# Sixty-four-row matmuls widened to 128 rows in a hybrid attention and convolution encoder

## The chip, the cores and the metric

The kernel runs on one core of a Trainium2 chip. The metric is the device time of one execution in microseconds; lower is better. On the core, TensorE multiplies (PE in the rows; its weight loads are listed apart, as PEld), VectorE (DVE), ScalarE (ACT) and GpSimd (POOL) work elementwise, SyncE (SP) issues the transfers, and 16 DMA engines carry them out.

## The reference

Two requests, of 512 and of 1024 tokens, pass through the same two layers:

```
h = rms_norm(x); proj = h @ w_in            # 1024 -> 3328 columns
q, k, v, g_a, u_h, g_h = split(proj)
attn: 8 query heads, 2 key heads, head size 64; q and k normalised and rotated
      s = q @ k.T * scale;  p = softmax(s);  o = p @ v
o_a = rms_norm(attn) * silu(g_a)
hyena: two long convolutions per channel, whose filters come from a small network:
      h = sin(fr * (z @ w1 + b1)); h = sin(fr * (h @ w2 + b2)); h = h @ w3   # 64 -> 2048
      h = h * (exp(-t * |decay|) + 0.05), normalised, then used through transforms
o_h = rms_norm(conv result) * silu(g_h)
x = x + concat(o_a, o_h) @ w_out
```

Two products have an inner size of 64: the scores `q @ k.T` (head size 64) and the third filter layer `h @ w3` (64 hidden units).

## The kernel before

Each operand of a product is kept as two 16-bit numbers, a high half and a low half (what the high half left over). A product of two such operands is three products of halves, high by high, high by low and low by high, added up in PSUM; low by low is left out.

Where the inner size is 64, the 128 partitions are used to do two of the three at once. `q_chunk` stores queries of key head g with their high half in the 64 partitions that start at g*64 and their low half in the other 64. `kv_chunk` stores the high half of each key head twice, one copy in each half of the partitions. So in `scores` the first matmul of a key block works on 128 rows (line 922: high and low queries by high keys), and the second on 64 rows alone (line 923: high queries by low keys). Line 923 occurs 320 times in the program. The third filter layer does the same in `filter_gen`, lines 801 and 802, with features stacked high over low and `w3_tile` giving the weights; line 802 occurs 96 times. All matmuls are issued by one helper, line 346, so all have that line in the rows. A row calls a matmul by its weight tile's rows and columns (`64*128` is a matmul on 64 rows) and by its moving operand (`64x512`).

The keys of one block of 512 tokens are built in `t16`, 12 tiles of 128x128 (four token tiles by three slots: head 0 high, head 1 high, low of both), and one transposing transfer on SP's queue (line 663) turns them into `kT`, 3 KB a partition. Queries go the same way with 16 tiles (line 629), softmax weights with 8 or 16 (line 945).

The work is cut into parts, which three threads walk through in a fixed order (`THREADS`): projections of both layers, filters and then attention, convolution and output of the long request, attention and the rest of the short one. `emit` writes the program down by turns from these threads, keeping an estimate of VectorE's work near a set ratio to TensorE's; each engine then works in that order. On-chip memory is handed out by `Arena` in pieces of 1 KB a partition, by age. When fewer than `ROOM` = 32 of its 202 KB are free, `emit` lets only the first thread go on (a thread that found itself waiting excepted):

```python
            tight = self.m.n - sum(self.m.used) < ROOM
            for t in order:
                if tight and n > 1 and t is not threads[0] and threads[0].last != "wait":
                    continue
```

Attention makes a tile of scores for 128 queries, takes its softmax (maximum on DVE, exponential on ACT, two halves on ACT and DVE, a transposing transfer), and multiplies by the values some tiles later.

Of the kernel before, what the change touches and what calls it, by code (L numbers as in the profile page):

```python
# [13 lines left out]
AF = mybir.ActivationFunctionType  # L14
ALU = mybir.AluOpType
AX = mybir.AxisListType.X

P = 128
# [11 lines left out]
RATIO = 0.85  # L30
# [17 lines left out]
# column offsets of the per-channel parameters  # L48
C_NW, C_CW, C_CB, C_DEC, C_HB, C_AW, C_HW, C_N = 0, 8, 44, 56, 72, 80, 84, 88

S_H = 2.0 ** 10      # normalised activations
S_W = 2.0 ** 8       # projection weights
S_QK = 2.0 ** 7      # q and k after rotation
S_V = 2.0 ** 8
S_P = 2.0 ** 14      # softmax weights
S_C = 2.0 ** 11      # transform matrices
S_F = 2.0 ** 13      # filters
S_OA = 2.0 ** 8      # gated attention output
S_OH = 2.0 ** 10     # gated hyena output
S_U = (2.0 ** 6, 2.0 ** 8)   # folded conv inputs  # L60
S_Y = (2.0 ** 5, 2.0 ** 7)   # spectra of conv outputs
S_W3 = 2.0 ** 10
# [79 lines left out]
class Arena:  # L142
    """On-chip memory in units of 1 KB a partition. A piece is taken that has been free for a while, small
    short-lived ones from the low end and the others from the high end; if there is none, the piece that has
    been free for longest."""
# [41 lines left out]
class Psum:  # L187
    """PSUM banks by class of use; in each class the banks free for longest are taken first."""
# [29 lines left out]
class Thread:  # L218
    """Parts of the work in their order, as steps."""
# [14 lines left out]
class Kern:  # L234
# [24 lines left out]
    def share(self, name, load):  # L259
        """Buffers that several threads read: loaded by the first, freed by the last."""  # L260
        if name not in self.shared:
            self.shared[name] = [load(), 0]
        self.shared[name][1] += 1
        return self.shared[name][0]
# [10 lines left out]
    def keep(self, n):  # L275
        """Columns that stay."""
        o = self.small_n
        self.small_n += n
        assert self.small_n <= 512
        return self.small[:, o:o + n]  # L280

    def tmp(self, n):
        """Columns that are soon used up."""
        if self.ring_n + n > 512:
            self.ring_n = 0
        o = self.ring_n
        self.ring_n += n
        return self.ring[:, o:o + n]
# [7 lines left out]
    def early(self, ap):  # L296
        """Instructions that free a PSUM bank go before others of their time."""
        return EVAC if ap.tensor is self.pt_tensor else 0
# [54 lines left out]
    def emit(self, threads):  # L353
        """Emit threads side by side, so that the work of VectorE keeps to RATIO times that of TensorE: by
        turns one whose present part loads TensorE more, or one whose present part loads VectorE more."""
# [31 lines left out]
    def rsqrt(self, out, ss, n, a, b):  # L387
        """out = (a * ss + b) ** -0.5 on [P, n] columns."""
        v, y, z = self.tmp(n), self.tmp(n), self.tmp(n)
        self.ts(v, ss, a, b, ALU.mult, ALU.add)  # L390
        yi = y.bitcast(I32)
        self.ts(yi, v.bitcast(I32), 1, None, ALU.logical_shift_right)
        self.ts(yi, yi, -1, 0x5F3759DF, ALU.mult, ALU.add)
        for i in range(3):
            self.tt(z, y, y, ALU.mult)
            self.stt(z, z, -0.5, v, ALU.mult, ALU.mult)
            self.stt(out if i == 2 else y, z, 1.5, y, ALU.add, ALU.mult)

# [18 lines left out]
    def sine(self, out, x, n):  # L417
        """out = sin(x) with x taken into [-pi, pi]."""
        b = self.m.alloc((n * 4 + 1023) // 1024)
        k = b.f32(n)  # L420
        magic = 12582912.0
        self.ts(k, x, 1.0 / (2 * math.pi), magic, ALU.mult, ALU.add)
        self.ts(k, k, magic, None, ALU.subtract)
        c1 = 6.28125
        c2 = float(np.float32(2 * math.pi - c1))
        for c in (c1, c2):
            self.stt(x, k, -c, x, ALU.mult, ALU.add)
        self.ts(x, x, 3.1415925, -3.1415925, ALU.min, ALU.max)
        self.act(out, x, AF.Sin)
        b.free()  # L430

    def features(self):
        """Hidden layers of the filter networks, one layer of the trunk in each half of the partitions;
        each is stored as a stack of a high and a low half."""
# [110 lines left out]
    def w_chunk(self, l, c0):  # L545
        """256 columns of w_in, scaled and split; the halves are kept in memory for the next use."""
# [19 lines left out]
    def tok_proj(self, l, w, blk, done):  # L566
        """Four token tiles of 256 output columns, handed to done two at a time."""
# [17 lines left out]
    def rotate(self, raw, nh, blk, kind):  # L585
        """raw [P, 4, nh * 64]: per-head RMS norm and rotation in place of the tile; returns its Buf."""
# [26 lines left out]
    def q_chunk(self, l, blks, g):  # L613
        """Four query heads of one key head."""
# [19 lines left out]
    def kv_chunk(self, l, blks):  # L634
        W, w = self.w_chunk(l, 512)
        m = self.m
        for blk in blks:
# [15 lines left out]
            tb = m.alloc(3)  # L653
            t16 = tb.f16(1536)
            for g in range(2):
                hi = V(t16, g * 128, [384, 4], [64, 2], [1, 64])
                src = V(rb.f32(512), g * 64, [128, 4], [0, 2], [1, 64])
                self.act(hi, src, AF.Copy, scale=S_QK)
                self.stt(V(t16, 256 + g * 64, [384, 4], [1, 64]), V(rb.f32(512), g * 64, [128, 4], [1, 64]), S_QK,
                         V(t16, g * 128, [384, 4], [1, 64]), ALU.mult, ALU.subtract)  # L660
            rb.free()
            kb = self.kT[l, blk] = m.alloc(3, True)
            self.q.dma_start_transpose(out=V(kb.f16(1536), 0, [P, 12], [1, P]), in_=t16)
# [4 lines left out]
    def ch_proj(self, l, w, c2, blk):  # L668
        """One tile of 128 output channels over one block of tokens."""
# [10 lines left out]
    def u_chunk(self, l, blks, j):  # L680
        """Short convolution of 256 channels."""
# [27 lines left out]
    def g_chunk(self, l, blks, j):  # L709
        """Gates, as silu times 2 * S_H * S_W."""  # L710
# [17 lines left out]
    def proj_q(self, l, s):  # L728
        """Queries, keys, values and their gates."""
# [11 lines left out]
    def proj_u(self, l, s):  # L741
        """Inputs of the convolutions and their gates."""
# [29 lines left out]
    def w3_tile(self, l, o, c):  # L772
        """Columns of filt_w3 for 128 channels, forward and backward; the high half twice, the low half once."""
# [6 lines left out]
        self.stt(w[0:64, 1], r[0:64], S_W3, w[0:64, 0], ALU.mult, ALU.subtract)  # L780
# [3 lines left out]
    def filter_gen(self, l, o, c, w3, F, t, L, t0):  # L784
        """Windowed filters of 128 channels, forward and backward, with their scale."""
        m = self.m
        out = []
        for dr in range(2):
# [7 lines left out]
            for i in range(L // 512):  # L796
# [5 lines left out]
                self.mm(p.ap, w3[0:64, 1, ch:ch + P], F[0:64, r], False, True)  # L802
# [79 lines left out]
    def attention(self, l, s):  # L882
        """Score tiles run one ahead of the softmax, products with V one behind it."""
# [31 lines left out]
    def scores(self, l, blks, qg, pr, j, qi):  # L915
# [3 lines left out]
        for i, kb in enumerate(blks):  # L919
            kt = self.kT[l, kb].f16(1536).rearrange("p (t s n) -> p t s n", t=4, s=3)  # L920
            o = s.ap[:, i * 512:(i + 1) * 512]
            self.mm(o, qv, kt[:, :, g], True, False)
            self.mm(o, qv[g * 64:g * 64 + 64], kt[g * 64:g * 64 + 64, :, 2], False, True)
        return s

    def softmax(self, s, PT, qi, nb):
        """Weights of one tile of 128 queries, normalised, split and transposed."""
# [20 lines left out]
    def values(self, l, blks, qg, pr, PT, sqs):  # L948
        """Weighted values of two heads for 256 queries, by channel, and their gate."""
# [34 lines left out]
    def gate_out(self, l, c, o, t0, n, sc, od, grp):  # L984
        """o [128 channels, n tokens] times its gate, split and stored for the output projection."""
# [53 lines left out]
    def conv_chain(self, l, s, c, CF, CI):  # L1039
        """Both convolutions of 128 channels of one sequence."""  # L1040
# [12 lines left out]
    def fold(self, u, dst, scale, nb):  # L1053
        """Sums and differences of the halves of each block about its middle, split and transposed."""
# [117 lines left out]
    def split(self, dst, y):  # L1172
        """High and low halves of y, which dst holds in its first free dimension."""
# [4 lines left out]
    def wo_tiles(self, l, grp):  # L1178
        """The rows of w_out of one group of heads, scaled and split."""
# [24 lines left out]
    def out_half(self, l, t, grp, x, sc, WO):  # L1204
        """x += sc * (gated group output) @ (its rows of w_out) for one token tile."""
# [15 lines left out]
    def out_attn(self, l, s):  # L1221
        """The attention heads' part of the output projection, added to the residual of one sequence."""
# [19 lines left out]
    def out(self, l, s):  # L1242
        """The other part of the output projection, and the norm that follows."""
# [75 lines left out]
def _layout(a):  # L1319
    """Per-channel parameters as columns, and the weights in the order of their loads."""  # L1320
# [32 lines left out]
```

## Time and profile before

| what | value |
|---|---|
| time, median of 3 runs | 2420.97 us (2419.26 to 2422.3) |
| profiled execution, first to last instruction (span) | 2406.2 us |
| instructions | 39740 |
| TensorE busy | 2061.8 us, 15436 matmuls, 15436 weight loads |
| VectorE busy | 1853.7 us |
| ScalarE busy | 1146.9 us |
| GpSimd busy | 432.0 us |
| mean granted TensorE clock | 0.940 of full speed |
| main DMA queue's packets | 78.6% of 16 engines' span |

The busy time of an engine is the time during which at least one of its instructions was under way. Matmuls overlap each other in the pipeline and their ends are modelled, so the distance from one start to the next says more than the duration of one.

### The profile page before, as it was taken

How to read it: one execution, taken by the hardware profiler on the slowest of the kernel's cores; microseconds unless marked ns; L12 is line 12 of the kernel's file. 1: busy time of each engine (PE TensorE's matmuls, PEld its weight loads, DVE VectorE, ACT ScalarE, POOL GpSimd, SP SyncE). 2: the span in 40 equal slices, each digit the busy share in tenths (PEclk: the TensorE clock that was granted, in tenths of full speed). 3: DMA queues.
4: the chain of work that ended last, by engine and by line, in shares of the span. 5: the costliest groups of instructions: out<-in, count | busy, mean ns of one | idle time of the engine just before them, and what ended most of it. 6: DMA issues, size and time to landing. Idle time of an engine off the chain costs nothing. (4 is left out here: it accounts for less than half of the span.)

```text
span 2406.2 us, 39740 instructions
## 1 busy us (share of the span) xinstructions
PE 2061.8 (86%) x15436; PEld 1249.0 (52%) x15436; DVE 1853.7 (77%) x3109; ACT 1146.9 (48%) x2016; POOL 432.0 (18%) x288
## 2 busy tenths in 40 slices
PE   5888889999989889878798778899999998887587
PEld 3656544444554556555575645444446445555453
DVE  7777677777767889976778767687777776998966
ACT  6545445766644234223544445366655652232322
POOL 1323120000110222222223312100011002222321
PEclk9899999999999899989899989999999999999789
DMA  8686659989999668688956678688989999574664
GB/s 230 151 209 174 166 152 216 225 187 203 230 253 265 189 171 215 193 260 266 222 137 191 169 184 215 177 195 192 225 187 197 225 264 305 173 202 118 204 203 136
DMA packets 774534, 485.86 MB, mean 202 GB/s; under 512 B 664838, under 2 KB 720295, under 8 KB 761288
## 3 DMA queue, kind: packets, MB, share of 16 engines
q1 hardware_dynamic: 773952, 482.96, 78.6%
q8 instruction: 121, 1.98, 0.3%
q14 instruction: 69, 0.57, 0.1%
q10 hardware_dynamic: 392, 0.34, 0.1%
HBM read 192.76 MB, written 139.20 MB: 138 GB/s over the span
## 5 line engine op out<-in xcount | busy, mean ns | idle before, releaser
L346 PE MATMUL psum<-arena 128*128 128x512 f16 (+4 forms) x15052 | 2018.5, 300 | 311.7 <-DMA arena<-arena 150.8
L346 PEld LDWEIGHTS <-arena 128*128 128x128 f16 (+2 forms) x15040 | 1199.0, 104 | 1087.5 <-issue 450.4
L328 POOL TENSOR_TENSOR arena<-arena 128x512 f32<-128x512 f32 (+4 forms) x218 | 415.2, 1912 | 1750.7 <-ACT arena L308 1032.4
L328 DVE TENSOR_TENSOR arena<-arena 128x1024 f32<-128x1024 f32 (+4 forms) x484 | 524.5, 1114 | 68.0 <-POOL arena L328 26.9
L308 ACT ACTIVATE arena<-arena 128x512 f16<-128x512 f32 (+4 forms) x359 | 265.1, 753 | 386.3 <-DVE arena L328 208.2
L320 DVE SCALAR_TENSOR_TENSOR arena<-arena,ring 128x1024 f16<-128x1024 f32 (+2 forms) x292 | 352.7, 1224 | 62.7 <-ACT arena L308 61.4
L308 ACT ACTIVATE arena<-psum 128x512 f32<-128x512 f32 (+2 forms) x336 | 177.2, 533 | 386.7 <-PE psum L346 380.6
L308 ACT ACTIVATE arena<-arena,ring 128x1024 f16<-128x1024 f32 (+1 forms) x280 | 287.2, 1044 | 148.9 <-DVE ring L939 29.8
L340 DVE TENSOR_REDUCE ring<-psum 128x1 f32<-128x1024 f32 (+1 forms) x192 | 197.5, 1039 | 55.6 <-PE psum L346 55.4
L308 ACT ACTIVATE arena<-arena,small 128x256 f16<-128x256 f32 (+5 forms) x288 | 167.2, 628 | 143.5 <-DMA arena<-in_p_win_dram 27.0
L320 DVE SCALAR_TENSOR_TENSOR arena<-psum,small,arena 128x511 f32<-128x511 f32 (+2 forms) x240 | 173.4, 743 | 63.8 <-PE psum L346 42.0
L320 DVE SCALAR_TENSOR_TENSOR arena<-psum,arena 128x512 f32<-128x512 f32 (+2 forms) x188 | 107.4, 598 | 129.7 <-ACT arena L308 121.0
L308 ACT ACTIVATE arena<-psum,ring 128x1024 f32<-128x1024 f32 (+1 forms) x192 | 185.6, 967 | 5.0 <-DMA g<-arena 0.5
L320 DVE SCALAR_TENSOR_TENSOR arena<-arena,small 128x256 f16<-128x256 f32 (+1 forms) x224 | 123.5, 583 | 22.9 <-ACT arena L308 15.2
L320 DVE SCALAR_TENSOR_TENSOR arena<-arena 128x512 f32<-128x512 f32 (+5 forms) x135 | 119.4, 890 | 11.7 <-ACT arena L308 11.1
L320 DVE SCALAR_TENSOR_TENSOR arena<-arena,psum 128x512 f32<-128x512 f32 (+1 forms) x144 | 95.6, 679 | 29.4 <-PE psum L346 15.2
L308 ACT ACTIVATE ring<-ring 128x1 f32<-128x1 f32 x192 | 37.4, 197 | 124.7 <-DVE ring L340 124.1
L334 DVE TENSOR_SCALAR ring<-ring 128x1 f32<-128x1 f32 (+8 forms) x339 | 61.1, 184 | 40.5 <-ACT arena L308 37.9
L308 ACT ACTIVATE arena<-psum,small 128x512 f32<-128x512 f32 x72 | 55.3, 771 | 53.7 <-PE psum L346 53.2
L346 PE MATMUL psum<-small,arena 128*128 128x1 f32 x384 | 56.5, 264 | 21.6 <-ACT arena L308 20.3
L346 PEld LDWEIGHTS psum<-small,arena 128*128 128x128 f32 x384 | 56.4, 218 | 33.9 <-ACT arena L308 24.2
L320 DVE SCALAR_TENSOR_TENSOR ring<-ring 128x16 f32<-128x16 f32 (+3 forms) x238 | 45.9, 194 | 5.0
(29 smaller groups left out, 262.9 us busy)
## 6 DMA issues: line engine op xcount, KB each, us to landing
f<-arena SPq DMA_DIRECT2D x128, 256.0 KB, 3.1
arena<-in_p_win_dram SPq DMA_DIRECT2D x26, 1024.0 KB, 6.2
w<-arena SPq DMA_DIRECT2D x26, 1024.0 KB, 4.7
arena<-w SPq DMA_DIRECT2D x26, 1024.0 KB, 6.1
arena<-f SPq DMA_DIRECT2D x16, 1536.0 KB, 7.4
u<-arena SPq DMA_DIRECT2D x24, 512.0 KB, 3.4
arena<-o SPq DMA_DIRECT2D x48, 256.0 KB, 4.2
y<-arena SPq DMA_DIRECT2D x24, 512.0 KB, 5.3
```

The lines of the kernel that those rows point to most:

```text
L308: r = self.s.activation(out=out, in_=in_, func=func, scale=scale, **kw)
L320: r = self.v.scalar_tensor_tensor(out=out, in0=a, scalar=sc, in1=b, op0=op0, op1=op1)
L328: r = (eng or self.v).tensor_tensor(out=out, in0=a, in1=b, op=op)
L334: return (eng or self.v).tensor_scalar(out=out, in0=a, scalar1=s1, scalar2=s2, op0=op0, **kw)
L340: r = self.v.tensor_reduce(out=out, in_=in_, op=op, axis=AX, **kw)
L346: return self.pe.matmul(out, lhsT, rhs, start=start, stop=stop)
```

## The change

Low halves are kept twice too, so that the third product also works on all 128 partitions. `t16` gets a fourth slot (the low half of each head in a slot of its own, in both halves of the partitions), `tb` and `kT` go from 3 to 4 KB, the transfer from 12 to 16 tiles, and one more ACT instruction a head copies the low half into the other 64 partitions' columns. In the filter the low half of `w3` is computed for all 128 rows, which already hold two copies. Lines 802 and 923 take all 128 rows; by that they also add low by low. The rest of the diff takes out comments and leaves the lines where they were.

```diff
@@ kv_chunk
-            tb = m.alloc(3)
-            t16 = tb.f16(1536)
+            tb = m.alloc(4)
+            t16 = tb.f16(2048)
             for g in range(2):
-                hi = V(t16, g * 128, [384, 4], [64, 2], [1, 64])
-                src = V(rb.f32(512), g * 64, [128, 4], [0, 2], [1, 64])
-                self.act(hi, src, AF.Copy, scale=S_QK)
-                self.stt(V(t16, 256 + g * 64, [384, 4], [1, 64]), V(rb.f32(512), g * 64, [128, 4], [1, 64]), S_QK,
-                         V(t16, g * 128, [384, 4], [1, 64]), ALU.mult, ALU.subtract)
+                src = V(rb.f32(512), g * 64, [128, 4], [1, 64])
+                hi, lo = (V(t16, (i * 2 + g) * 128, [512, 4], [1, 64]) for i in range(2))
+                self.act(V(t16, g * 128, [512, 4], [64, 2], [1, 64]), V(rb.f32(512), g * 64, [128, 4], [0, 2], [1, 64]), AF.Copy, scale=S_QK)
+                self.stt(lo, src, S_QK, hi, ALU.mult, ALU.subtract)
+                self.act(V(t16, (2 + g) * 128 + 64, [512, 4], [1, 64]), lo, AF.Copy)
             rb.free()
-            kb = self.kT[l, blk] = m.alloc(3, True)
-            self.q.dma_start_transpose(out=V(kb.f16(1536), 0, [P, 12], [1, P]), in_=t16)
+            kb = self.kT[l, blk] = m.alloc(4, True)
+            self.q.dma_start_transpose(out=V(kb.f16(2048), 0, [P, 16], [1, P]), in_=t16)
@@ w3_tile
-        self.stt(w[0:64, 1], r[0:64], S_W3, w[0:64, 0], ALU.mult, ALU.subtract)
+        self.stt(w[:, 1], r, S_W3, w[:, 0], ALU.mult, ALU.subtract)
@@ filter_gen
                 self.mm(p.ap, w3[:, 0, ch:ch + P], F[:, r], True, False)
-                self.mm(p.ap, w3[0:64, 1, ch:ch + P], F[0:64, r], False, True)
+                self.mm(p.ap, w3[:, 1, ch:ch + P], F[:, r], False, True)
@@ scores
-            kt = self.kT[l, kb].f16(1536).rearrange("p (t s n) -> p t s n", t=4, s=3)
+            kt = self.kT[l, kb].f16(2048).rearrange("p (t s n) -> p t s n", t=4, s=4)
             self.mm(o, qv, kt[:, :, g], True, False)
-            self.mm(o, qv[g * 64:g * 64 + 64], kt[g * 64:g * 64 + 64, :, 2], False, True)
+            self.mm(o, qv, kt[:, :, 2 + g], False, True)
```

## Rows read from the trace of the kernel before

**Rows 1.** Page, part 1: busy us (share of the span) x instructions.

```profile
PE 2061.8 (86%) x15436; PEld 1249.0 (52%) x15436; DVE 1853.7 (77%) x3109; ACT 1146.9 (48%) x2016; POOL 432.0 (18%) x288
```

**Rows 2.** Windows: length, busy (x) of PE PEld DVE ACT POOL, clock, DMA share, GB/s.

```profile
0.00:300.00 300.00, 236.66 (x2044) 164.89 (x2045) 226.63 (x447) 160.06 (x258) 69.79 (x65) 0.91 0.75 186
300.00:800.00 500.00, 460.44 (x3041) 242.03 (x3038) 366.32 (x655) 284.49 (x520) 52.35 (x39) 0.97 0.93 219
800.00:1500.00 700.00, 573.00 (x4753) 387.39 (x4752) 557.76 (x893) 293.55 (x494) 169.17 (x108) 0.92 0.74 198
1500.00:2000.00 500.00, 469.63 (x3047) 238.84 (x3044) 364.10 (x682) 295.38 (x566) 40.58 (x35) 0.99 0.88 209
2000.00:2406.00 406.00, 322.10 (x2559) 215.83 (x2559) 338.88 (x434) 113.39 (x178) 100.12 (x41) 0.91 0.62 190
```

**Rows 3.** Counts of the 64-row form in 300 to 800, then 1500 to 2000 us.

```profile
L346 PE MATMUL psum<-arena 64*128 64x512 f16 x157 | 60.7, 387 | 0.0
...
L346 PE MATMUL psum<-arena 64*128 64x512 f16 x166 | 64.2, 387 | 0.0
```

**Rows 4.** Chain that ended last: its first piece; by line, 1500 to 2000, 2000 to 2406.

```profile
1444.52 4.56 DVE arena L320 x2
...
by line: PE psum L346 58.6%; DMA arena<-arena 14.6%; DVE arena L320 9.0%; ACT arena L308 3.9%; DMA arena<-in_p_win_dram 2.6%; DVE ring L340 1.8%; issue 1.7%; SPq L945 1.5%; DMA f<-arena 1.2%; DMA u<-arena 0.9%; DMA arena<-u 0.9%; DVE arena 
...
by line: DVE arena L328 37.6%; PE psum L346 23.1%; DVE arena L320 11.7%; issue 7.4%; DMA arena<-f 5.7%; DMA arena<-arena 4.7%; ACT arena L308 3.0%; POOL arena L328 2.2%; DVE ring L320 1.2%; DMA arena<-o 0.8%; DVE ring L328 0.7%; DMA u<-aren
```

**Rows 5.** Groups by form, whole span: busy us, mean ns | idle before, releasers.

```profile
L346 PE MATMUL psum<-arena 128*128 128x512 f16 x4448 | 1104.1, 386 | 58.3 <-DVE arena L320 21.2 <-ACT arena L308 15.9 <-DMA arena<-o 7.6
L346 PEld LDWEIGHTS <-arena 128*128 128x128 f16 x12704 | 1043.2, 102 | 850.1 <-issue 248.5 <-ACT arena L308 50.8 <-DVE arena L328 31.8
...
L346 PE MATMUL psum<-arena 64*128 64x512 f16 x416 | 163.2, 393 | 0.0
...
L346 PEld LDWEIGHTS <-arena 64*128 64x128 f16 x416 | 38.4, 93 | 157.2 <-issue 156.2 <-DVE ring L334 0.4
...
L308 ACT ACTIVATE arena<-arena 128x256 f16<-128x256 f32 x64 | 26.1, 409 | 23.4 <-DVE arena L320 12.5 <-issue 5.5 <-DMA arena<-in_filt_w_dram 3.0
...
L320 DVE SCALAR_TENSOR_TENSOR arena<-arena 64x256 f16<-64x256 f32 x16 | 7.5, 470 | 1.0 <-ACT arena L308 1.0
...
L320 DVE SCALAR_TENSOR_TENSOR arena<-arena 128x256 f16<-128x256 f32 x12 | 5.0, 420 | 4.4 <-ACT arena L308 4.1
```

**Rows 6.** Timeline of matmuls, one unbroken run of a single form.

```profile
1006.24 2.10 PE L346 MATMUL psum<-arena 128*128 128x512 f16 x9
```

**Rows 7.** Timeline of weight loads in attention: start us, length, instruction, idle before.

```profile
1618.01 0.10 PEld L346 LDWEIGHTS <-arena 128*128 128x128 f16 x1 [0.23 <-issue]
1618.33 0.09 PEld L346 LDWEIGHTS <-arena 64*128 64x128 f16 x1 [0.23 <-issue]
1618.65 0.11 PEld L346 LDWEIGHTS <-arena 128*128 128x128 f16 x2 [0.23 <-issue]
```

**Rows 8.** Timeline of weight loads while filters are made.

```profile
189.21 0.09 PEld L346 LDWEIGHTS <-arena 64*128 64x128 f16 x1 [0.32 <-issue]
189.53 0.55 PEld L346 LDWEIGHTS <-arena 128*128 128x128 f16 x6 [0.23 <-issue]
```

**Rows 9.** Waits, whole span: total us, times, longest.

```profile
ACT arena L308 <- DVE arena L320: 133.6, 83, 5.6
```

**Rows 10.** Line 663, key transfers: issue ns min/median/max, who waited, landing us.

```profile
L663 SPq DMA_TRANSPOSE arena<-arena x6: 1481/2028/2410, 67.2 to 1838.2; - x6
...
ACT arena L308: 1.7, 1
...
DMA to landing us min/median/max: 4.0/6.1/6.8
```

**Rows 11.** Line 629, query transfers of 16 tiles: issue ns, landing us.

```profile
L629 SPq DMA_TRANSPOSE arena<-arena x12: 1322/2872/5727, 136.5 to 1905.5; - x12
...
DMA to landing us min/median/max: 4.3/4.8/9.1
```

## The prediction

> **What bounds the kernel now.** I read the busy shares first, then the windows by stage, then the chain of waits, and last the timeline of single weight loads. The shares name no sole bound: TensorE is busy 2061.8 us and VectorE 1853.7 of a span of 2406.2 [rows 1]. The windows show stages with different limits [rows 2]. In the two stretches where attention of the long request runs beside projections, 300 to 800 and 1500 to 2000 us, TensorE is busy 460 and 470 of 500 us and VectorE 366 and 364: there TensorE leads, with 30 to 40 us of true idleness. From 800 to 1500 both are near 80%, and at the end VectorE leads. Of the 416 matmuls on 64 rows, 157 and 166 lie in the two TensorE-led stretches [rows 3]; the other 93 lie before 300 us and from 800 to 1500, most of them in the filters.
>
> Busy is not the same as deciding. The chain of waits, which the trace follows back no further than 1444 us, says how much of a stretch TensorE decides: 58.6% between 1500 and 2000 us, and 23.1% at the end [rows 4]. Transposing transfers (14.6%) and VectorE take most of the rest of the attention stretch, and while the chain passes through them TensorE is mostly busy with something that nothing waits for. A saving there becomes a wait.
>
> **What a 64-row matmul costs.** The group rows mislead here: 393 ns for one on 64 rows against 386 for one on 128 [rows 5]. That is a modelled time through the pipeline, which says nothing of how soon the next starts. The reader should look at starts. A run of nine 128-row matmuls over 512 columns takes 2.10 us in all [rows 6]; less one duration of 0.386 that leaves eight steps of 0.214 us. In the scores the loads alternate 128, 64, 128 rows and start at 1618.01, 1618.33 and 1618.65 [rows 7]: steps of 0.32 us, with an idle 0.23 us before each load that is put down to "issue" and to no other engine. In the filters the step behind a 64-row load is again 0.32 us (189.21 to 189.53) [rows 8]. So both the step into 64 rows and the step out of them cost 0.32 instead of 0.214 us, and one 64-row matmul costs 2 x 0.32 - 2 x 0.214 = 0.21 us more than one on 128 rows would. The group of loads agrees: 156 us of idle "issue" stand before 416 loads of 64 rows, 0.375 us each [rows 5], which includes the normal gap.
>
> Some switches stand beside a wait, which hides them, so I take 0.20 us: 416 x 0.20 = 83 us of TensorE time. The bounds are 0 (the wider matmul might keep the long step) and 416 x 0.21 = 87.
>
> **Two readings of the 0.32 us.** It could be a weight load that nothing covers: 0.102 us for a load [rows 5] and 0.214 for the columns make 0.316. Or it could be a price of changing between 128 and 64 rows. In the unbroken run above every matmul has a load of its own, since loads and matmuls are equal in number [rows 1], and it still steps at 0.214 us, so between matmuls of one shape the load is covered. The widened matmuls have that shape, so I take the second reading; the first is a rival below. The Trainium skill, TensorE: Matmul & The Clock Gate, Part 3 (The mechanism), speaks for the first: a weight load overlaps a matmul in flight only where the row groups differ. By that rule the step of equal shapes would be 0.316 us and the change would give nothing; the plain run at 0.214 us disagrees. The same skill, TensorEngine Tiling (Array Packing), Key Properties, speaks for the second: changing the tiling mode drains TensorE. By that rule the sum stays as it is, and the 0.32 us on both sides of a 64-row matmul agree.
>
> **The parts.**
> - *Lines 923 and 802 on 128 rows*: 83 us less on TensorE. On the path: 323 matmuls in the attention stretches are 64.6 us. TensorE decides 58.6% of a stretch in which it is busy 93.9%, so 0.586 / 0.939 = 0.62 of its work is on the chain [rows 2, 4]. The chain is not shown for 300 to 800 us; its busy shares are within 2 points of the other's, and I use the same 0.62. That is 64.6 x 0.62 = 40.3 us. For the 93 others, 18.6 us, the nearest chain is that of the last, mixed stretch: 0.231 / 0.793 = 0.29 [rows 2, 4], so 5.4 us. Together 45.7.
> - *The copies of the low keys*: six calls of the key part (three blocks, two layers) with two copies each, 12 ACT instructions. The nearest row, 256 columns to 16 bits, has 0.409 us [rows 5], so 4.9 us of ACT. Each copy also waits for VectorE's low half (0.42 us, [rows 5]) while the next head's high half and the evacuation of projection banks stand behind it on ACT; a wait of ACT for this line of VectorE is 133.6 / 83 = 1.6 us on average [rows 9]. The upper bound is 12 x (0.41 + 1.6) = 24 us, the lower 0. ACT has 3.9% of the chain [rows 4] and is under 60% busy in every stage [rows 2], which hides nearly all of it: I take 2 us. Without that cover it would be the 24.
> - *The key transfer*, 12 to 16 tiles: the query transfers have just that size and land in 4.8 us against 6.1 for the keys [rows 10, 11], so no price for size can be seen in the landing. SP's issue takes 2.87 us against 2.03 [rows 10, 11]: 6 x 0.84 = 5 us more on SP's queue, in front of whatever the program issues next. Only one wait, of 1.7 us by ACT, hangs on the key transfers [rows 10], and SP's queue has 1.5% of the chain [rows 4]: 0, at most 5.
> - *VectorE's low half of w3* on 128 instead of 64 partitions: 0.47 us now, and 0.42 for 256 columns on 128 partitions [rows 5]; 16 instructions, 0 give or take 1 us.
> - *Memory*: 1 KB more for each key block, while blocks are live. It changes where pieces lie and when the order of emission thinks memory tight. No row prices it; see the last rival.
>
> The sum is -45.7 + 2 = -43.7 us. The profiled span of 2406.2 becomes 2362.5. Between that span and the median of the runs, 2421.0, lie 14.8 us outside the first and last instruction, which I keep: 2377 us.
>
> **The rivals.**
> - *All of it arrives.* If TensorE's order alone sets the pace, as its 92 to 94% in the attention stretches could mean, 83 us are saved less the 2: 2340 us. Against it are the 14.6% of transfers and 9% of VectorE on the chain [rows 4].
> - *It turns into waits.* Scores come earlier, but the softmax chain and its transposing transfer set when values may start. DMA engines are busy 0.93 and 0.88 of the attention stretches [rows 2], the highest of all stages, so transfers asked for sooner may land no sooner. If only a quarter of the 83 us arrives, 2421 - 21 + 2 = 2402 us; if none, 2421. For it: the chain is the first-order limit, and as soon as TensorE is shorter another path may take over. Against it: VectorE has 134 us of slack in each of these stretches.
> - *The long step stays.* If the 0.32 us is a load without cover, it stays for rows of any number, 416 x 0.20 us of saving is 0, and the 2 us of copies remain: 2423 us. The plain run at 0.214 us [rows 6] speaks against it. The rule of the Trainium skill, TensorE: Matmul & The Clock Gate, Part 3, would have it so.
> - *Slower: the threads lose their cover.* Key blocks of 4 KB bring the free memory under 32 KB sooner, from where on only the first thread is written down. If attention is held back and later runs with as little beside it as the work from 800 to 1500 us, where TensorE is busy 573 of 700, the 460 us of TensorE work of one attention stretch take 460 / 0.819 = 562 us instead of 500: 62 us more, 2377 + 62 = 2439 us. It decides the sign from 44 / 62, some 0.7 of one stretch. For it: the rule compares against a fixed limit, so 1 KB can tip it. Against it: a few KB in 202.
>
> **How the numbers follow.** Chances: the forecast 0.62, all of it 0.13, waits 0.12, the long step 0.04, slower 0.09. What tells from no change is about 0.2%, 4.8 us. Of the waits I put three quarters below 2416 us, so faster is 0.62 + 0.13 + 0.09 = 0.84; same 0.03 + 0.04 = 0.07; slower 0.09. The range has to leave out at most 0.2: I cut at 2412 above, which leaves out slower, the long step and a third of the waits (0.17), and at 2334 below, which takes in the full 87 us (2421 - 87 = 2334).
>
> **What would show it.** Right: no form with 64 rows is left, 4448 + 416 = 4864 matmuls of the 128x512 form, loads of the scores at steps of 0.214 us, TensorE's busy time down by about 80 us, VectorE's unchanged near 1854, and more TensorE idle behind transposing transfers, some 35 to 40 us in all. Wrong in the first step: score loads still at 0.32 us. Wrong in the second: TensorE's busy time down by 80 but the span by under 20 (waits) or by over 70 (all of it). Wrong in the last part: an attention stretch with fewer projection matmuls beside it and a TensorE share nearer 82%.

## The result and the profile after

The changed kernel takes 2438.64 us (median of 4 runs, 2437.43 to 2439.88) against 2420.11 for the kernel before: a ratio of 1.0082, interval 1.0061 to 1.0103. It is slower by 0.8%, where 1.8% faster was forecast; the time lies outside the range of 2334 to 2412.

One number needs a word: in the changed kernel's profiled run the span is 2437.1 us and the run 2438.89, so only 1.8 us lie outside the span, not the 14.8 of the prediction. By that, the span of 2406.2 before belongs to an execution of about 2408 us, 12 below its median; below, medians and ratios are compared, not spans.

The page's first part and, by form, the groups that answer to those of [rows 5]:

```profile
PE 2011.0 (83%) x15436; PEld 1275.4 (52%) x15436; DVE 1868.0 (77%) x3109; ACT 1147.5 (47%) x2026; POOL 424.7 (17%) x288
```

```profile
L346 PE MATMUL psum<-arena 128*128 128x512 f16 x4864 | 1168.7, 390 | 92.6 <-ACT arena L308 39.2 <-DVE arena L320 26.2 <-DMA arena<-h 10.0
L346 PEld LDWEIGHTS <-arena 128*128 128x128 f16 x13120 | 1108.2, 103 | 974.8 <-issue 262.6 <-ACT arena L308 51.5 <-DMA arena<-arena 47.9
...
L308 ACT ACTIVATE arena<-arena 128x256 f16<-128x256 f16 x12 | 4.3, 404 | 0.4 <-DVE arena L320 0.4
```

All 4448 + 416 matmuls are of one form now. The 12 copies of the low keys take 4.3 us of ACT, and ACT was idle 0.4 us ahead of them: they did not hold it up. The next row is TensorE's timeline in the second attention stretch, a run of 24 matmuls in which a key block pair's four score matmuls stand in the middle:

```profile
1621.79 5.34 PE L346 MATMUL psum<-arena 128*128 128x512 f16 x24
```

Its weight loads stand beside it one by one, 24 of them:

```profile
1621.68 4.95 PEld L346 LDWEIGHTS <-arena 128*128 128x128 f16 x24
```

Less one duration, the 24 matmuls make 23 steps of (5.34 - 0.39) / 23 = 0.215 us: the steps of 0.32 us of [rows 7] are gone. TensorE's busy time is down by 51 us (2061.8 to 2011.0), not by about 80; the two kernels' orders differ, and a comparison within one order comes below. So the first step of the prediction holds in kind, and the kernel is slower all the same. The windows by stage (columns as in [rows 2]) say where:

```profile
0.00:300.00 300.00, 227.48 (x2054) 164.96 (x2055) 228.67 (x449) 158.31 (x259) 70.20 (x66) 0.93 0.74 190
300.00:800.00 500.00, 430.49 (x3029) 248.01 (x3027) 365.94 (x652) 286.71 (x524) 50.04 (x38) 0.95 0.95 220
800.00:1500.00 700.00, 550.48 (x4556) 379.99 (x4556) 548.18 (x854) 278.01 (x472) 161.37 (x101) 0.89 0.69 189
1500.00:2000.00 500.00, 448.69 (x3100) 250.87 (x3099) 364.45 (x681) 296.26 (x557) 43.37 (x39) 0.98 0.88 207
2000.00:2437.10 437.10, 353.88 (x2701) 231.57 (x2699) 360.71 (x475) 128.22 (x215) 99.70 (x44) 0.89 0.63 191
```

Count matmuls, since both kernels have 15436. At 800 us the changed kernel has started 2054 + 3029 = 5083, the one before 2044 + 3041 = 5085 [rows 2]: level, although TensorE is busy 30 us less in the attention stretch. From 800 to 1500 us it starts 4556 against 4753 and is then 199 behind, with transfers down from 0.74 to 0.69 and the granted clock from 0.92 to 0.89. The loss appears in the stretch with few of the changed matmuls. That is no sign of a dearer product, and it is not where the prediction's slower rival put it either.

TensorE's idle time behind transposing transfers, first in the kernel before:

```profile
PE psum L346 <- DMA arena<-arena: 150.8, 73, 8.1
```

Then in the changed kernel, with ACT's wait behind VectorE's low halves ([rows 9] for before):

```profile
PE psum L346 <- DMA arena<-arena: 191.6, 86, 7.0
ACT arena L308 <- DVE arena L320: 180.8, 99, 15.8
```

The first grows by 41 us, about as the prediction said (35 to 40). The second was 133.6 us, with a longest wait of 5.6; the copies don't make its growth, since they waited 0.4 us in all. The key transfers land in 5.0 us (6.1 before, [rows 10]), and no TensorE wait hangs on them:

```profile
  POOL arena L328: 10.7, 1
  ACT arena L308: 7.5, 2
...
DMA to landing us min/median/max: 4.3/5.0/6.5
```

### The profile page after: what moved, and what is told of

Same layout as the page of the kernel before. It is cut to its first block, busy times and chain, and to the rows that moved or that the text cites. A ratio compares the mean times of both kernels' runs of the same rounds, so it can differ in the third digit from the quotient of the medians.

```text
span 2437.1 us, 39814 instructions
## 1 busy us (share of the span) xinstructions
PE 2011.0 (83%) x15436; PEld 1275.4 (52%) x15436; DVE 1868.0 (77%) x3109; ACT 1147.5 (47%) x2026; POOL 424.7 (17%) x288
## 5 line engine op out<-in xcount | busy, mean ns | idle before, releaser
L346 PE MATMUL psum<-arena 128*128 128x512 f16 (+4 forms) x15052 | 1968.8, 302 | 386.0 <-DMA arena<-arena 191.6
L346 PEld LDWEIGHTS <-arena 128*128 128x128 f16 (+1 forms) x15040 | 1226.0, 105 | 1083.3 <-issue 308.4
L328 POOL TENSOR_TENSOR arena<-arena 128x512 f32<-128x512 f32 (+4 forms) x218 | 407.7, 1876 | 1841.4 <-ACT arena L308 1162.7
L308 ACT ACTIVATE arena<-arena 128x512 f16<-128x512 f32 (+5 forms) x371 | 269.1, 742 | 424.8 <-DVE arena L328 212.2
L320 DVE SCALAR_TENSOR_TENSOR arena<-arena 128x512 f32<-128x512 f32 (+4 forms) x135 | 126.8, 944 | 11.7 <-ACT arena L308 10.2
```

The lines of the kernel that those rows point to most:

```text
L308: r = self.s.activation(out=out, in_=in_, func=func, scale=scale, **kw)
L320: r = self.v.scalar_tensor_tensor(out=out, in0=a, scalar=sc, in1=b, op0=op0, op1=op1)
L328: r = (eng or self.v).tensor_tensor(out=out, in0=a, in1=b, op=op)
L346: return self.pe.matmul(out, lhsT, rhs, start=start, stop=stop)
```

## The experiments

Two facts of the programs come first. The order of the parts that `emit` writes is the same in both kernels, step for step, and the rule for tight memory never acts: counted while the program is written, at most 147 of the 202 KB are in use after a step (145 before). But between `emit` and the engines stands a scheduler, which lays each engine's instructions out by what they depend on; the description ahead of the prediction left it out. Larger key pieces move most later buffers, a buffer at another place waits for another earlier user, and the engines' orders differ from the first projections on. All kernels below are named by what they do; those that are called of one order have the same instructions in the same order on every engine. Times are medians; ratios are to the kernel before, run on the same chip in between.

### The widening without the layout, and the layout without the widening

```diff
# scores alone, in place: kt keeps three slots
-            self.mm(o, qv[g * 64:g * 64 + 64], kt[g * 64:g * 64 + 64, :, 2], False, True)
+            self.mm(o, qv, kt[:, :, 2], False, True)
```

> Line 923 alone is widened to 128 rows, on the third key slot as it is: its other 64 partitions hold the low keys of the other head, so low queries times the low keys of the wrong head are added; nothing else is changed, every engine's instructions stand in the order of before, and no buffer moves. Three theories of the changed kernel's 2439 us. Placement: the widening gains, and the 4 KB key pieces lose more by moving every later buffer and so the order of instructions; then this kernel gains 320 x 0.20 us x about 0.62, some 40 us: 2370 to 2390. Waits: the saved TensorE time comes back as waiting whatever the placement; then 2410 to 2425. Work: the added copies and the larger key transfers cost; then it gains as under placement.

Measured: 2411.36 us, ratio 0.9952 (0.9932 to 0.9971), in the order of before. It gains 11 us, not 40; the 64 us that the expectation starts from (320 x 0.20) are 47 in the busy times, 2061.8 - 2015.1, of two executions. The page's first part:

```profile
PE 2015.1 (83%) x15436; PEld 1270.9 (53%) x15436; DVE 1853.9 (77%) x3109; ACT 1144.0 (47%) x2016; POOL 431.3 (18%) x288
```

TensorE's wait for the softmax's transposing transfers (line 945) grows, first the kernel before, then this one:

```profile
  PE psum L346: 42.0, 27
```

```profile
  PE psum L346: 80.1, 43
```

```diff
# scores and filter, in place
+            self.mm(o, qv, kt[:, :, 2], False, True)
+        self.stt(w[:, 1], r, S_W3, w[:, 0], ALU.mult, ALU.subtract)
+                self.mm(p.ap, w3[:, 1, ch:ch + P], F[:, r], False, True)
```

> Lines 923 and 802 are widened and w3's low half is computed for 128 rows; the keys stay in three slots, so low queries times the low keys of the wrong head are added in the scores. A few instructions change places near the filters. Placement and work: 5 to 15 us below the kernel with the scores alone widened, 2360 to 2385. Waits: 2410 to 2425.

Measured: 2410.01 us, ratio 0.9946 (0.9928 to 0.9964): faster than both kernels, and the filters add next to nothing.

```diff
# the changed kernel, products on 64 rows again
-            self.mm(o, qv, kt[:, :, 2 + g], False, True)
+            self.mm(o, qv[g * 64:g * 64 + 64], kt[g * 64:g * 64 + 64, :, 2 + g], False, True)
-                self.mm(p.ap, w3[:, 1, ch:ch + P], F[:, r], False, True)
+                self.mm(p.ap, w3[0:64, 1, ch:ch + P], F[0:64, r], False, True)
```

> The changed kernel with its copies, its four slots, its 4 KB pieces and its order, but lines 923 and 802 on 64 rows again. Placement and work: slower than the changed kernel by what widening gives, 20 to 60 us: 2460 to 2500. Waits: within 10 us of the changed kernel, 2430 to 2450, since widening gives nothing.

Measured: 2458.35 us, ratio 1.0149 (1.0121 to 1.0177). It has the order of the changed kernel, so the pair says what widening is worth there: 1.0149 - 1.0082 = 0.0067, 16 us. That lies between the two theories, which asked for 20 to 60 us and for at most 10. Its TensorE is busy 2081.9 us, 71 more than the changed kernel's 2011.0, 0.17 us for each of the 416 matmuls:

```profile
PE 2081.9 (85%) x15436; PEld 1249.0 (51%) x15436; DVE 1872.3 (76%) x3109; ACT 1150.0 (47%) x2026; POOL 424.6 (17%) x288
```

```diff
# the kernel before with larger pieces and nothing else
-            tb = m.alloc(3)
+            tb = m.alloc(4)
-            kb = self.kT[l, blk] = m.alloc(3, True)
+            kb = self.kT[l, blk] = m.alloc(4, True)
```

> The kernel before, computing and moving exactly what it did, but its key pieces and their source take 4 KB instead of 3, with the last KB unused. Placement: much slower than before by placement alone, 2455 to 2500. Work: as before, 2415 to 2430, since no copy and no tile is added. Waits: as before, 2415 to 2430.

Measured: 2464.37 us, ratio 1.0168 (1.014 to 1.0196). No copy, no tile, no product was changed, and the whole loss is there and more. The added work is not the cause; with it and 64 rows the time was 2458.35. Its window from 800 to 1500 us reads like the changed kernel's:

```profile
800.00:1500.00 700.00, 553.22 (x4501) 378.02 (x4498) 552.15 (x847) 270.07 (x455) 167.73 (x102) 0.89 0.68 185
```

### Is it the larger pieces, or any other placement?

```diff
-ARENA_KB = 202
+ARENA_KB = 201   # and 203, 198; in the kernel before, the changed one, and others
```

> The kernel before with an arena of 201 KB instead of 202: the same instructions, the same sizes of pieces, and other addresses for most of them. If the loss of the 4 KB pieces is that any other placement than the one of before is slower (before lies at the fast end), this too loses 20 to 50 us: 2440 to 2475. If the loss is special to the larger key pieces (memory is short, or a piece waits for its neighbour), this stays at 2410 to 2430.

Measured: 2443.56 us, ratio 1.008 (1.0056 to 1.0105), in the range set for a loss by any other placement.

> The same with 203 KB, one more than before. Any other placement is slower: 2440 to 2475. Special to the larger pieces: 2410 to 2430; if memory is short, at or below 2420.

Measured: 2429.93 us, ratio 1.0023 (1.0005 to 1.0041). That is in the range set for a loss special to the larger pieces, at its upper end, and below that set for any other placement; the next runs settle it.

> The changed kernel with an arena of 203 KB instead of 202: the same work at other addresses. If the changed kernel's place is an ordinary draw and each placement is worth some plus or minus 20 us, this lies anywhere from 2410 to 2460, and not at the same 2439. If the larger pieces themselves cost, it stays at 2430 to 2445.

Measured: 2418.66 us, ratio 0.9978 (0.9959 to 0.9997): with one KB more to choose from, the change is not slower.

> The changed kernel with an arena of 198 KB instead of 202, as a third draw of its places beside 2439 and 2419 us. If places are a draw worth plus or minus 20 us: 2400 to 2450, and not below what less memory must cost. If less memory costs: above 2440.

Measured: 2411.39 us, ratio 0.9967 (0.9945 to 0.9988), with 4 KB less.

> Lines 923 and 802 widened on three key slots (low queries times the low keys of the wrong head are added), arena of 203 KB. Without widening this arena gave 2430; the widening gains 11 to 20 us in every order so far: 2405 to 2420.

Measured: 2422.47 us, ratio 1.0007 (0.9988 to 1.0027), slightly above the expected range; 0.0016, 4 us, below the kernel with 203 KB and no widening, of one order with it, which is not clear of the noise. The changed kernel at 203 KB, widened too but with the layout, has 0.9978: there the layout costs nothing, it is 0.0029, 7 us, faster, though the intervals touch.

> The kernel before with an arena of 198 KB: a further draw of the places of its 3 KB key pieces, and the base of the next. 2415 to 2450.

Measured: 2462.0 us, ratio 1.0163 (1.0133 to 1.0194), above the range.

> The changed kernel's layout (copies, four key slots, 4 KB pieces) with the products on 64 rows, arena of 198 KB; its instructions stand in the same order as in the changed kernel with 198 KB, which took 2411. If the layout itself costs about 40 us wherever the pieces lie, this is 35 to 45 us above the kernel before with 198 KB. If that cost at 202 KB was a draw, the distance lies between minus 25 and plus 25. Against the changed kernel with 198 KB it shows the widening's gain once more: 10 to 25 us.

Measured: 2422.04 us, ratio 0.9999 (0.9979 to 1.0019). At 198 KB the same layout is 1.6% faster than the old one, 40 us, more than the 25 expected of a draw; at 202 KB it was 1.5% slower. So no price of the layout shows through the placement: its cost goes from 36 us to minus 40 with the size of the arena. Against the changed kernel at 198 KB, of one order with it but for two transfers on SP's queue that change places, the widening is worth 0.9999 - 0.9967 = 0.0032, 8 us, below the expected 10 to 25; the intervals overlap. The windows up to 1500 us, first of the kernel before at 198 KB, then of the layout:

```profile
0.00:300.00 300.00, 228.62 (x1912) 157.47 (x1913) 227.49 (x445) 155.93 (x253) 70.19 (x64) 0.92 0.70 180
300.00:800.00 500.00, 457.92 (x3047) 238.70 (x3045) 356.27 (x651) 285.90 (x519) 42.81 (x38) 0.96 0.93 213
800.00:1500.00 700.00, 553.59 (x4608) 380.89 (x4606) 551.25 (x856) 279.84 (x470) 159.51 (x103) 0.90 0.72 195
```

```profile
0.00:300.00 300.00, 230.09 (x1967) 159.08 (x1968) 224.74 (x442) 157.47 (x257) 67.02 (x65) 0.91 0.72 184
300.00:800.00 500.00, 457.66 (x3117) 239.72 (x3115) 366.34 (x659) 289.63 (x526) 49.50 (x39) 0.99 0.94 223
800.00:1500.00 700.00, 574.93 (x4676) 388.69 (x4676) 551.44 (x880) 287.56 (x488) 162.32 (x106) 0.90 0.71 194
```

Again the slower one has TensorE busy some 20 us less from 800 to 1500 us. But here most of its lag is older: it has started 4959 matmuls at 800 us against 5084, 125 behind, and at 1500 us it is 193 behind. So the stretch in which a placement loses its time changes with the placement. All draws with products on 64 rows: 2421, 2443, 2430, 2462 us with 3 KB pieces (202, 201, 203, 198 KB), and 2464, 2458, 2422 with 4 KB (two at 202, one at 198). The kernel before stands at the fast end, level with one other of the seven, and the spread is 40 us.

### How much of TensorE's time counts

To vary TensorE's time alone, each score matmul is cut into halves of 256 columns. The order high, low, low, high has one change of rows and back a key block; high, low, high, low has two; on 128 rows there is none. The three are of one order.

```diff
+            self.mm(o[:, 0:256], qv, kt[:, 0:2, g], True, False)
+            self.mm(o[:, 0:256], qv[g * 64:g * 64 + 64], kt[g * 64:g * 64 + 64, 0:2, 2], False, True)
+            self.mm(o[:, 256:512], qv[g * 64:g * 64 + 64], kt[g * 64:g * 64 + 64, 2:4, 2], True, False)
+            self.mm(o[:, 256:512], qv, kt[:, 2:4, g], False, True)
```

> The kernel before with each score matmul cut into two of 256 columns, in the order high, low, low, high, so that rows change from 128 to 64 and back once a key block, as before. The base for the next two, which have the same instructions in the same order on every engine. The cut itself changes the order against before, worth up to 2%: 2400 to 2470.

Measured: 2439.36 us, ratio 1.006 (1.0041 to 1.008).

> The same order, with the low products on all 128 rows (low queries times the low keys of the wrong head are added): no change of rows, some 64 us less of TensorE than with one change. If most of the saved time comes back as waits, 10 to 20 us below the kernel with one change; if the 0.62 of the chain held, 35 to 45 us below.

Measured: 2419.0 us, ratio 0.997 (0.9954 to 0.9986): 20 us below.

> The same instructions on 64 rows, in the order high, low, high, low: rows change twice a key block, some 64 us more of TensorE than with one change. If TensorE is one of several paths of nearly the same length, more of an added microsecond counts than of a saved one: 25 to 50 us above the kernel with one change. If TensorE simply is hidden by something else, 5 to 20 us above.

Measured: 2455.24 us, ratio 1.0128 (1.0104 to 1.0152): 16 us above. Busy times of the three pages, none, one and two changes:

```profile
PE 2024.1 (84%) x16076; PEld 1327.9 (55%) x16076; DVE 1852.4 (77%) x3109; ACT 1148.0 (47%) x2016; POOL 426.0 (18%) x288
```

```profile
PE 2090.3 (86%) x16076; PEld 1276.0 (53%) x16076; DVE 1861.1 (77%) x3109; ACT 1149.6 (47%) x2016; POOL 423.2 (17%) x288
```

```profile
PE 2135.3 (87%) x16076; PEld 1295.1 (53%) x16076; DVE 1870.0 (76%) x3109; ACT 1149.7 (47%) x2016; POOL 417.7 (17%) x288
```

TensorE's busy time differs by 66 and 45 us, the time by 20 and 16: 0.31 and 0.35 of it. An added microsecond counts about as much as a saved one, so the expectation of a steeper side was wrong. One reading is that TensorE is on the deciding path in about a third of the places where it changes rows. The rest turns into waits or comes out of waits, 31 of 46 us and 26 of 29 by the rows below; TensorE's idle time behind transposing transfers, in the same order:

```profile
PE psum L346 <- DMA arena<-arena: 174.8, 85, 7.7
```

```profile
PE psum L346 <- DMA arena<-arena: 143.7, 69, 8.3
```

```profile
PE psum L346 <- DMA arena<-arena: 118.1, 61, 7.6
```

### What takes the rest

```diff
# products with V one score tile later
-            if late:
-                late()
-                late = None
-                yield
+            if late:
+                wait_ -= 1
+                if wait_ == 0:
+                    late()
+                    late = None
+                    yield
             if j == 1 and qi == 1:
-                late = lambda a=(l, blks, qg, pr, PT, sqs): self.values(*a)
+                late, wait_ = (lambda a=(l, blks, qg, pr, PT, sqs): self.values(*a)), 2
```

> The kernel before, with the products with V of each group of four score tiles written one score tile later, so that the softmax and its transposing transfer have longer before TensorE needs them. The order changes throughout, and with it the time, by up to 2% either way: 2400 to 2470. It serves as the base for the next kernel, which has the same order on every engine.

Measured: 2440.57 us, ratio 1.0066 (1.0045 to 1.0088).

> The kernel with the products with V later, and line 923 on 128 rows in place (low queries times the low keys of the wrong head are added). If the widening gained only 11 us of 64 in the order of before because the products with V then wait for the transposing transfers of the softmax, it gains more where these have longer: 30 to 50 us below the kernel with 64 rows and late products. If the gain is lost elsewhere (clock, VectorE, other loads), the distance stays at 5 to 20 us.

Measured: 2427.14 us, ratio 1.0019 (1.0003 to 1.0036): 0.0047, 11 us below its base, as much as in the order of before. TensorE's wait for the softmax's transfers (line 947 in these two) is less than half of what it was above, first with 64 rows, then with 128:

```profile
  PE psum L346: 18.9, 12
```

```profile
  PE psum L346: 33.6, 20
```

More time for these transfers does not let the gain through.

```diff
# high halves of the softmax weights alone are transposed and used
-        self.q.dma_start_transpose(out=V(PT.f16(2 * KT * 256), qi * P, [256, 2 * KT], [1, P]), in_=hb.f16(2 * L))
+        self.q.dma_start_transpose(out=V(PT.f16(2 * KT * 256), qi * P, [256, KT], [1, P]), in_=hb.f16(L))
-                    self.mm(o[j * 64:j * 64 + 64], vb[:, vh, k % 4, g * 64:g * 64 + 64], pt[:, ph, k], n == 0, n == 3 * KT - 1)
+                    self.mm(o[j * 64:j * 64 + 64], vb[:, vh, k % 4, g * 64:g * 64 + 64], pt[:, 0, k], n == 0, n == 3 * KT - 1)
```

> The kernel before with only the high halves of the softmax weights transposed and used (the products take the high half in place of the low one; the low half is still computed): the softmax's transposing transfers are half as large, TensorE's and VectorE's work is the same. If these transfers set the pace of the attention stretches, it is 40 to 100 us faster than before. If VectorE's and ScalarE's part of the softmax sets it, it stays at 2400 to 2450, as any other order does. It is the base of the next kernel.

Measured: 2399.98 us, ratio 0.9915 (0.9885 to 0.9946). The transfers' share in the attention stretch falls from 0.93 [rows 2] to 0.75, and the kernel is 20 us faster than before, half of the least that was expected if they set the pace. Its order differs from that of before, so part of this may be a draw (against the other orders with 64 rows, 2421 to 2464 us, it is 20 to 60):

```profile
300.00:800.00 500.00, 469.92 (x3222) 248.58 (x3220) 386.87 (x680) 295.59 (x540) 53.00 (x42) 0.98 0.75 191
```

> The same, same order, with line 923 on 128 rows in place (low queries times the low keys of the wrong head are added). If the widening's gain is taken by waits for the transposing transfers, it grows with these halved: 30 to 50 us below the kernel with 64 rows. If it is taken by whatever path is next, it stays at 10 to 20.

Measured: 2386.73 us, ratio 0.985 (0.9809 to 0.9892): 0.0065, 16 us below its base, within the 10 to 20 expected if another path takes the gain. Yet TensorE's added idle time still ends at transposing transfers, 64 rows first:

```profile
PE psum L346 <- DMA arena<-arena: 138.8, 61, 8.4
```

```profile
PE psum L346 <- DMA arena<-arena: 163.3, 77, 8.2
```

So shortening these transfers does not let the gain through, although the waits that take it end there. That they wait in turn for the softmax ahead of them is likely, but no run shows it.

## Why the prediction was wrong

**The price of a change of rows was right.** The runs of equal form step at 0.215 us, the long steps left with the 64-row form, and in each of eight pairs of one order the kernel with fewer changes of rows is the faster one, by 4 to 22 us by the ratios (in three of them, at 198 KB, at 203 KB and with the high halves alone, the intervals overlap). Its sum was somewhat large: the 416 matmuls were to give 83 us of TensorE time and gave 71 in one order. The rival in which the long step stays has fallen: 24 matmuls on all rows, each with a load, step at 0.215 us. By the Trainium skill, TensorE: Matmul & The Clock Gate, Part 3 (The mechanism), a load overlaps matmuls in flight only where the row groups differ; these 24 disagree. The Trainium skill, TensorEngine Tiling (Array Packing), Key Properties, says that a change of tiling mode drains TensorE; the 0.32 us that vanished agrees.

**Its share on the path was too large.** The prediction took 0.62 for the attention stretches, from TensorE's share of the chain that ended last in one execution. The widening of the scores gave 11 us in the order of before, 0.24 of the 47 us of busy time, and 16 of 71 in the order of the changed kernel, 0.23; the kernels with halves have 0.31 and 0.35, the pair at 203 KB 0.05 (4 of 78, 2075.0 to 1996.8). The likely reason, which no run shows, is that a chain names one path among several of almost the same length and puts each step down to whoever came last, so that near-ties count in full. The prediction's rival of waits had the size about right: a quarter of 83 us.

**The step that failed and turned the sign is "Memory: no row prices it", which the sum took as nothing.** The larger pieces alone cost 42 us at 202 KB (2464 against 2423 in the same session) and the full layout 36; the widening then gives 16 to 20 back, which makes the measured 18 above the kernel before. The slower rival named the right place in the code, the 4 KB pieces, and by chance the time, 2439 us; but its mechanism did not happen. Memory never ran tight, no thread lost its cover in the attention stretches, and the loss at 202 KB came from 800 to 1500 us. What happens instead is that buffers lie elsewhere, so dependences through reused memory and the order that the scheduler makes of them differ. The same layout loses 1.5% at 202 KB, wins 1.6% at 198 and costs nothing at 203, and a change of 1 KB in the arena alone cost the kernel before 0.8%.

**The small terms held.** Copies: 12 x 0.404 us of ACT with 0.4 us of idle time ahead of them. Key transfers: they land as fast as before and TensorE never waits for them. VectorE's w3 term can't be told from nothing.

**What stays open**: which of the reused buffers cost the time, and why a gain in TensorE's time counts 0.05 in one order and 0.35 in another. Only the sum of a placement was measured, not one dependence, and placement and order were not told apart, since the one makes the other.

## What to carry to other kernels

A matmul on 64 rows between matmuls on 128 costs TensorE 0.2 us more than a wide one here, and filling the other 64 partitions with data that are there anyway, without new buffers, was the version that gained at 202 KB (0.54%); in the scores those data are the low keys of the other head, so small products are added that the result does not ask for. In this kernel, whose TensorE, VectorE and ScalarE are busy 86, 77 and 48% of the span, a microsecond taken from TensorE was worth 0.05 to 0.35, in most orders a fifth to a third, where one chain said 0.62. Where a change alters the size of a buffer in a packed arena, compare it with the old kernel at several placements before believing either sign: the draw, 40 us here, was larger than the effect.

## What was not expected of the hardware

TensorE's mean granted clock falls a little where its work shrinks. Over all executions of each kernel, the mean is lower with fewer changes of rows in seven of the eight pairs of one order, by 0.001 to 0.005, and level in the eighth (0.932, the scores alone in place). In the kernels with halves, the profiled executions have 0.939 with one change of rows and 0.932 with none:

```profile
core 0: 2430.1 us, clock 0.939
```

```profile
core 0: 2417.2 us, clock 0.932
```

This pair shows more than the usual difference: over ten executions each, the means are 0.936 and 0.933. With two levels, 2.4 and 1.2 GHz, a mean of 0.936 is 12.8% of the span at the lower one, 0.128 x 2438 = 312 us, and 0.933 is 0.134 x 2417 = 324 us: some 12 us more, an estimate. The kernel with less work for TensorE leaves it idle longer behind transfers (174.8 against 143.7 us above). That this is why the clock falls, and that it takes back part of the saving, is likely but not shown: no row says how much of the added time at the lower level is work.
